# A fourth k-pair by seven block products in four of ten pairs of the second feed-forward's up stage, with a second k-pair's remainders there by ScalarE and adding DMAs

## The chip, the cores and the metric

The kernel runs on one NeuronCore of a Trainium2 chip. The metric is device time in microseconds (us) of one execution; the kernel before takes 2561.94 us, the median of three runs (2561.91 to 2562.84). A NeuronCore has a tensor engine (PE) for matmuls, a vector engine (DVE), a scalar engine (ACT), GpSimd (POOL) and SyncE (SP). Each runs its own instructions in order and waits on semaphores for the others. SP and POOL issue DMAs here; those of POOL can add to what lies at their destination.

## The reference

One layer of a diffusion backbone: a half-step SwiGLU, a mixing of tokens by attention and a long convolution, and another half-step SwiGLU, over 256 latent tokens (and 256 context tokens up to the mixing). The change is in the last SwiGLU, the second feed-forward:

```python
D_MODEL = 2048
SEQ = 256
D_FF = 5632

def swiglu(h, w_up, w_down):
    gate, up = jnp.split(h @ w_up, 2, axis=-1)
    return (jax.nn.silu(gate) * up) @ w_down

def half_ffn(s, m, slot, g, w_up, w_down):
    h = modulate(rms_norm(s, g), chunk(m, 3 * slot), chunk(m, 3 * slot + 1))
    return s + 0.5 * chunk(m, 3 * slot + 2) * swiglu(h, w_up, w_down)
```

All of it is in float32. Here `h` is 256 x 2048 and `w_up` 2048 x 11264.

## The kernel before

**Three matmuls for one.** The operands of PE are cast to `F32R`. To keep the precision, each operand x is split into a cast `hi` and a remainder `lo` = x - hi, and a product is hi·hi + lo·hi + hi·lo: three matmuls, added up in PSUM (`tok_mm`). The stationary operand is a 128 x 128 piece of the activations, the moving one 512 columns of weights. ACT makes the casts of the weights and DVE the remainders, in the order that `in_turn` writes down for each engine.

**The up stage.** The columns of `w_up` are taken in groups of 256 up columns with their 256 gate columns. Groups 0 and 1 come first, each alone (the loop `for g in range(2)`); the rest are ten pairs p = 1 to 10 of two groups. `plan` lists the pairs with their eight k-pairs q = 0 to 7 (a k-pair is 256 of the 2048 input rows), and after them the down stage. The loop over `plan` loads and splits the next k-pair's weights (`quad_of(*plan[n + 1])`) ahead of the matmuls of this one (`multiply`).

**Two ways to multiply a k-pair.** Plain: the tokens are two blocks of 128, the inner rows two, the columns two of 512; 8 block products of three matmuls, 24 in all. Block products (`is_summed`): seven in place of eight, 21 matmuls, of which some multiply sums of blocks. The sums of activation blocks are made once for each k-pair (`combine`, at group 1); those of weight blocks each time: `quad` subtracts in place in the raw tiles and then casts and takes remainders of four things, the first block (`first`, in the tiles `sq`, of which there is one pair), and `plain`, `odd` and `even` of two blocks each. Before, q = 2, 4 and 6 (`SUMMED`) are done so in pairs 1 to 10 (`SUM_PAIRS`). Four PSUM banks `mixed` hold products that enter several results; `collect` brings them together behind the last of these k-pairs, and `gated` applies the gate.

**Remainders by DMA.** For q = 1 of pairs 2 to 10 (argument `by_dma` of `quad`) DVE makes no remainder: ACT writes -hi into the tile `lo` (L1670), and a DMA issued by POOL adds the raw weights to it (L1671).

**Buffers.** The raw tiles (`raw`, `vraw`) are a ring of six, three k-pairs deep. The split tiles (`whi` and `wlo`, `vhi` and `vlo`) are a ring of five units; a plain k-pair takes two of them and one of block products three, beside the pair `sq`. A unit is filled again when PE has read the one five units back. The order of each engine's instructions is made by a scheduler that goes by when it believes operands to be ready; `in_turn` and `issue_after` bind it for casts and remainders of weights.

After the matmuls of q = 1 PE transposes the gated activations of the pair before (`turn_act`, L1598), which ACT and DVE split and, for some groups, POOL writes to DRAM (L1601, L1610).

Of the kernel before, what the change touches and what calls it, by code (L numbers as in the profile page):

```python
# [29 lines left out]
UPG = FF // 256  # L30
# [40 lines left out]
def hybrid_layer_kernel(ctx: ExitStack, tc: tile.TileContext, a):  # L71
# [20 lines left out]
    def tmp2(shape):  # L92
        return T(up, shape, "sg", bufs=3)
# [123 lines left out]
    def split(src, shape):  # L217
        hi, lo = U(shape, F32R), U(shape, F32R)
        S.copy(hi, src)
        V.tensor_sub(lo, src, hi.bitcast(F32))  # L220
        return hi, lo

    def split_to(src, hi, lo):
        S.copy(hi, src)
        V.tensor_sub(lo, src, hi.bitcast(F32))
        return hi, lo
# [1367 lines left out]
    def turn_act(g, at, bank=PB):  # L1594
# [8 lines left out]
        acts[g] = split(pt, (P, 2, L)) if g in SPILLED else split_to(pt, act_tile(), act_tile())  # L1603
        if g in DOWN_SUMMED[0]:
            m_ = tmp2((P, 2, L))
# [139 lines left out]
    for g in range(2):  # L1745
        ps = groups[g]
        behind = None
        if g == 0:
            for t in range(2):
                for ps_, ws_ in zip(groups, (ws, ws1)):  # L1750
                    for k in range(4):
                        tok_mm(ps_, [h[k][:, s, :] for s in range(2)], ws_[k], k == 0, False, (t,))
                if t == 0:
                    pt = turned(xn)
                    for d in range(4):
                        hi, lo = mod2(d, pt[:, d, :], h[d][:, :, P:L])
                        behind = behind or (lo, hi)
            rest_h(1)
        for kp in range(8):
            if kp < 2:  # L1760
                continue
            if g == 0 and kp == 2:
                pieces = ws[4:6]
            else:
                late = dict(zip(("behind", "behind_hi"), behind)) if g == 0 and kp < 6 else {}
                whi, wlo = weight(a["w_up2"][g, kp], (P, 2, 512), **late)
                pieces = [(whi[:, k2, :], wlo[:, k2, :]) for k2 in range(2)]
            for k2 in range(2):
                k = 2 * kp + k2
                tok_mm(ps, [h[k][:, s, :] for s in range(2)], pieces[k2], k == 0, k == KT - 1)  # L1770
            if g == 0 and kp in (2, 4):
                rest_h(kp // 2 + 1)
            if kp == 2 and prev:
                turn_act(*prev)
            if g == 0 and kp == 5:
                for t in range(2):
                    for b in range(NB):
                        nc.gpsimd.dma_start(xtd[t][b], xt[t][b])
            if g == 1 and kp in (3, 4, 5):
                combine(SUMMED[kp - 3])  # L1780
        at = U((P, 2, L))
        for t in range(2):
            sg = tmp2((P, L))
            S.activation(sg, ps[t][:, 0:L], AF.Silu)
            V.tensor_mul(at[:, t, :], ps[t][:, L : 2 * L], sg)
        prev = (g, at)
# [1 line left out]
    plan += [(UPG // 2 + bp, g) for bp in range(2) for g in DOWN_ORDERS[bp]]  # L1788

    def is_summed(p, q):  # L1790
        return q in DOWN_SUMMED[p - UPG // 2] if p >= UPG // 2 else p in SUM_PAIRS and q in SUMMED

    def quad_of(p, q):
        src = a["w_up2p"][p - 1] if p < UPG // 2 else a["w_dn2p"][p - UPG // 2]
        return quad([src[2 * q + k2] for k2 in range(2)], is_summed(p, q), p in SUM_PAIRS[1:] and q == 1)

    def fetch_next(at, count):

# [189 lines left out]
```

## Time and profile before

| | |
|---|---|
| median of three runs | 2561.94 us |
| profiled execution | 2561.77 us, span 2560.0 us |
| mean granted clock of PE | 0.997 |
| DVE | 2161.7 us busy, 84% |
| ACT | 1218.1 us busy, 48% |
| POOL | 367.1 us busy, 14% |

An engine's busy time is the union of its instructions; matmuls overlap, so a row's duration is longer than the distance to the next. In the table of stretches the span is cut at chosen times, here at the first matmuls of the pairs. In the chain of waits the last instruction is followed back to what released it. A timeline's row ends with a bracket where its engine was idle: how long, and whose end released it. "x2" joins two instructions of a kind that follow each other.

### The profile page before, as it was taken

What the parts mean: (1) busy time and instruction counts of PE and PEld (TensorE: products, weight loads), DVE (VectorE), ACT (ScalarE), POOL (GpSimd) and SP (SyncE); (2) the same over time, 40 slices, a digit from 0 to 9 for tenths busy, and PEclk for the clock granted to TensorE, in tenths of its full rate; (3) what the DMA queues carried; (4) which work ended last, traced back from release to release, by engine and by line L of the source; (5) the groups of instructions that cost most, each with busy time, mean ns of one, the idle gap of its engine ahead of it and who ended that gap; (6) DMA issues with size and microseconds to landing.
All of it is one profiled execution on the core that took longest, in us unless ns stands there. A gap on an engine that the chain in (4) does not pass through costs nothing.

```text
span 2560.0 us, 38554 instructions
## 1 busy us (share of the span) xinstructions
PE 2546.0 (99%) x14245; PEld 2191.0 (86%) x14245; DVE 2161.7 (84%) x3488; ACT 1218.1 (48%) x1710; POOL 367.1 (14%) x590
## 2 busy tenths in 40 slices
PE   8999999999999999999999999999999999999999
PEld 5678999999999999888888988888888888888887
DVE  6777888888888886777989797889789999999998
ACT  5454444444444443111211355567566666665554
POOL 1122222222222223320011000000000011012010
PEclk8999999999999999999999999999999999999999
DMA  9997888888888889996798556545747778789784
GB/s 362 389 284 221 250 243 254 242 245 243 252 247 256 245 251 314 395 372 204 257 333 294 187 158 183 161 127 164 250 160 238 232 255 256 245 256 315 235 286 158
DMA packets 209530, 641.27 MB, mean 250 GB/s; under 512 B 24603, under 2 KB 27644, under 8 KB 204988
## 3 DMA queue, kind: packets, MB, share of 16 engines
q1 hardware_dynamic: 134252, 481.84, 55.4%
q0 software_dynamic: 74896, 156.83, 23.7%
q8 instruction: 111, 1.82, 0.3%
q14 instruction: 79, 0.65, 0.1%
q10 hardware_dynamic: 192, 0.13, 0.0%
HBM read 559.25 MB, written 48.53 MB: 237 GB/s over the span
## 4 chain that ended last, share of the span: by engine, by line
PE 98%; DMA 1%; DVE 0%; ACT 0%; issue 0%; SPq 0%; ACTq 0%; DVEq 0%
PE pb L255 10%; PE pb L256 9%; PE pb L257 9%; PE pa L255 9%; PE pa L256 9%; PE pa L257 9%; PE pa L1418 6%; PE pa L1420 6%; PE pa L1419 6%; PE pb L1418 4%; PE pb L1420 4%; PE pb L1419 4%; PE pa L263 3%; PE pa L265 2%; PE pa L1105 1%; PE pa L1106 1%
## 5 line engine op out<-in xcount | busy, mean ns | idle before, releaser
L244 ACT CAST whi<-raw 128x1024 fp32r<-128x1024 f32 x233 | 245.1, 1052 | 480.9 <-PE pb L256 194.7
L248 DVE TENSOR_TENSOR wlo<-raw,whi 128x1024 fp32r<-128x1024 f32 x233 | 284.2, 1221 | 120.7 <-ACT whi L244 120.3
L255 PE MATMUL pa<-u,whi 128*128 128x256 f32 (+1 forms) x912 | 307.1, 337 | 2.1 <-ACT u L903 2.1
L256 PE MATMUL pa<-u,whi 128*128 128x256 f32 (+1 forms) x912 | 304.8, 334 | 0.4 <-DVE u L908 0.4
L257 PE MATMUL pa<-u,wlo 128*128 128x256 f32 (+1 forms) x912 | 304.5, 334 | 0.0
L255 PE MATMUL pb<-u,whi 128*128 128x256 f32 (+1 forms) x904 | 300.4, 332 | 0.0
L256 PE MATMUL pb<-u,whi 128*128 128x256 f32 (+1 forms) x904 | 298.5, 330 | 0.0
L257 PE MATMUL pb<-u,wlo 128*128 128x256 f32 (+1 forms) x904 | 298.3, 330 | 0.0
L467 ACT CAST bhi<-raw 128x768 fp32r<-128x768 f32 x111 | 92.5, 833 | 267.6 <-PE pb L256 131.8
L159 DVE CUSTOM_DVE_ANT_0 adas<-adaw,crow,cond 128x1024 bf16<-128x1024 f32 x160 | 204.9, 1280 | 14.3 <-DMA adaw<-in_w_adaT_dram 12.6
L159 DVE CUSTOM_DVE_ANT_0 adas<-adaw,crow,mod 128x1024 bf16<-128x1024 f32 x160 | 204.9, 1281 | 12.0 <-DMA adaw<-in_w_adaT_dram 10.0
L255 PEld LDWEIGHTS pa<-u,whi 128*128 128x128 f32 x912 | 173.1, 190 | 24.8 <-issue 4.1
L256 PEld LDWEIGHTS pa<-u,whi 128*128 128x128 f32 x912 | 173.5, 190 | 17.5 <-DVE u L908 1.5
L257 PEld LDWEIGHTS pa<-u,wlo 128*128 128x128 f32 x912 | 173.5, 190 | 17.1
L470 DVE TENSOR_TENSOR blo<-raw,bhi 128x768 fp32r<-128x768 f32 x111 | 106.2, 957 | 94.6 <-ACT bhi L467 94.4
L255 PEld LDWEIGHTS pb<-u,whi 128*128 128x128 f32 x904 | 171.8, 190 | 16.2 <-issue 0.7
L257 PEld LDWEIGHTS pb<-u,wlo 128*128 128x128 f32 x904 | 171.8, 190 | 15.6
L256 PEld LDWEIGHTS pb<-u,whi 128*128 128x128 f32 x904 | 171.9, 190 | 15.4
L278 ACT CAST whi<-raw 128x1024 fp32r<-128x1024 f32 x122 | 126.9, 1052 | 98.9 <-DVE raw L278 65.0
L1420 PE MATMUL pa<-whi,u 128*128 128x512 f32 x443 | 172.5, 389 | 0.0
L1418 PE MATMUL pa<-whi,u 128*128 128x512 f32 x442 | 172.5, 392 | 0.0
L1419 PE MATMUL pa<-wlo,u 128*128 128x512 f32 x442 | 172.2, 390 | 0.0
(473 smaller groups left out, 6673.5 us busy)
## 6 DMA issues: line engine op xcount, KB each, us to landing
adaw<-in_w_adaT_dram SPq DMA_DIRECT2D x224, 512.0 KB, 5.8
raw<-in_w_up1q_dram SPq DMA_DIRECT2D x124, 512.0 KB, 5.0
raw<-in_w_up2p_dram SPq DMA_DIRECT2D x107, 512.0 KB, 4.8
raw<-in_w_dn_dram SPq DMA_DIRECT2D x94, 512.0 KB, 5.6
u<-act POOLq DMA_DIRECT2D x172, 256.0 KB, 9.8
wrow<-in_w_ada_dram SPq DMA_DIRECT2D x32, 1024.0 KB, 10.9
raw<-in_w_dn2p_dram SPq DMA_DIRECT2D x59, 512.0 KB, 5.3
vraw<-in_w_up2p_dram SPq DMA_DIRECT2D x53, 512.0 KB, 5.0
```

The source lines that it names most:

```text
L159: V.tensor_tensor_reduce(out=sc, in0=t, in1=crow[i][:, b * (D // 2) : (b + 1) * (D // 2)], scale=1.0, scalar=mcol if b else bada[:, c * KT ...
L244: last_hi[0] = S.copy(hi, raw)
L248: last_lo[0] = V.tensor_sub(lo, raw, hi.bitcast(F32))
L255: PE.matmul(ps, w[0], xx[0], start=start, stop=False)
L256: PE.matmul(ps, w[0], xx[1], start=False, stop=False)
L257: return PE.matmul(ps, w[1], xx[0], start=False, stop=stop)
L278: return do(*args, **kw)
L467: return raw, hi, lo, S.copy(hi, raw[:, :, 0:3])
L470: return V.tensor_sub(lo, raw[:, :, 0:3], hi.bitcast(F32))
L1418: PE.matmul(ps[t], hi, w[0], start=start, stop=False)
L1419: PE.matmul(ps[t], hi, w[1], start=False, stop=False)
L1420: last = PE.matmul(ps[t], lo, w[0], start=False, stop=stop)
```

## The change

k-pair 5 joins 2, 4 and 6 in pairs 3, 5, 7 and 9, so that q = 4, 5 and 6 are block products one after the other there; `combine` makes its activation sums at group 1. In the same pairs the remainders of q = 3 are made by ACT and DMA, as those of q = 1 are.

```diff
+FOURTH, FOURTH_PAIRS = 5, range(3, 11, 2)
...
-            if g == 1 and kp in (3, 4, 5):
-                combine(SUMMED[kp - 3])
+            if g == 1 and kp in (3, 4, 5, 6):
+                combine((SUMMED + (FOURTH,))[kp - 3])
...
     def is_summed(p, q):
-        return q in DOWN_SUMMED[p - UPG // 2] if p >= UPG // 2 else p in SUM_PAIRS and q in SUMMED
+        return q in DOWN_SUMMED[p - UPG // 2] if p >= UPG // 2 else p in SUM_PAIRS and (q in SUMMED or q == FOURTH and p in FOURTH_PAIRS)
 
     def quad_of(p, q):
         src = a["w_up2p"][p - 1] if p < UPG // 2 else a["w_dn2p"][p - UPG // 2]
-        return quad([src[2 * q + k2] for k2 in range(2)], is_summed(p, q), p in SUM_PAIRS[1:] and q == 1)
+        return quad([src[2 * q + k2] for k2 in range(2)], is_summed(p, q), p in SUM_PAIRS[1:] and (q == 1 or q == 3 and p in FOURTH_PAIRS))
```

The new line near the top moves every line behind it down by one: L278 before is L279 after. The rows below show what stands in the engines' queues in pair 5. DVE before, from the last remainder of q = 4 through the two remainders of q = 5 to the chain of q = 6 (`sq` the first block, `raw` and `vraw` the raw tiles, `lo` tiles the remainders):

```order
L278 TENSOR_TENSOR vlo_21255<-raw_21246,vhi_21254 128x1024
L278 TENSOR_TENSOR vlo_21297<-raw_21292,vhi_21296 128x1024
L278 TENSOR_TENSOR wlo_21301<-vraw_21294,whi_21300 128x1024
L278 TENSOR_TENSOR sq_21330<-vraw_21325,sq_21329 128x512
L278 TENSOR_TENSOR vraw_21325<-vraw_21325 128x512
L278 TENSOR_TENSOR vraw_21325<-raw_21327,vraw_21325 128x512
L278 TENSOR_TENSOR wlo_21332<-raw_21327,whi_21331 128x1024
L278 TENSOR_TENSOR raw_21327<-raw_21327,vraw_21325 128x512
L278 TENSOR_TENSOR raw_21327<-raw_21327 128x512
L278 TENSOR_TENSOR wlo_21334<-vraw_21325,whi_21333 128x1024
L278 TENSOR_TENSOR vlo_21336<-raw_21327,vhi_21335 128x1024
```

DVE after, from the last remainder of q = 4 through the whole chain of q = 5 to the start of that of q = 6:

```order
L279 TENSOR_TENSOR vlo_21280<-raw_21271,vhi_21279 128x1024
L279 TENSOR_TENSOR sq_21322<-raw_21317,sq_21321 128x512
L279 TENSOR_TENSOR raw_21317<-raw_21317 128x512
L279 TENSOR_TENSOR raw_21317<-vraw_21319,raw_21317 128x512
L279 TENSOR_TENSOR wlo_21324<-vraw_21319,whi_21323 128x1024
L279 TENSOR_TENSOR vraw_21319<-vraw_21319,raw_21317 128x512
L279 TENSOR_TENSOR vraw_21319<-vraw_21319 128x512
L279 TENSOR_TENSOR wlo_21326<-raw_21317,whi_21325 128x1024
L279 TENSOR_TENSOR wlo_21328<-vraw_21319,whi_21327 128x1024
L279 TENSOR_TENSOR sq_21367<-vraw_21362,sq_21366 128x512
L279 TENSOR_TENSOR vraw_21362<-vraw_21362 128x512
L279 TENSOR_TENSOR vraw_21362<-raw_21364,vraw_21362 128x512
```

The two remainders between the chains are gone and eight instructions stand in their place; the three chains of q = 4, 5 and 6 touch each other.

PE before, the last rows of q = 6 in pair 5 (tiles `pa` and `pb` are PSUM banks, `u` activations and their sums):

```order
L1418 MATMUL pa_21209<-whi_21333,u_19509 128x512
L1419 MATMUL pa_21209<-wlo_21334,u_19509 128x512
L1420 MATMUL pa_21209<-whi_21333,u_19510 128x512
L1418 MATMUL pb_21083<-vhi_21335,u_19296 128x512
L1419 MATMUL pb_21083<-vlo_21336,u_19296 128x512
L1420 MATMUL pb_21083<-vhi_21335,u_19296 128x512
L1418 MATMUL pa_21208<-vhi_21335,u_19509 128x512
L1419 MATMUL pa_21208<-vlo_21336,u_19509 128x512
L1420 MATMUL pa_21208<-vhi_21335,u_19510 128x512
```

PE after, the same place:

```order
L1419 MATMUL pb_21106<-whi_21372,u_19296 128x512
L1420 MATMUL pa_21233<-vlo_21371,u_19509 128x512
L1421 MATMUL pa_21233<-vhi_21370,u_19510 128x512
L1420 MATMUL pa_21232<-vlo_21371,u_19509 128x512
L1421 MATMUL pa_21232<-vhi_21370,u_19510 128x512
L1419 MATMUL pa_21231<-whi_21372,u_19509 128x512
L1420 MATMUL pb_21106<-wlo_21373,u_19296 128x512
L1421 MATMUL pb_21106<-whi_21372,u_19296 128x512
L1420 MATMUL pa_21231<-wlo_21373,u_19509 128x512
L1421 MATMUL pa_21231<-whi_21372,u_19510 128x512
```

Before, each product's three matmuls stand together. After, the scheduler puts the ones that read only casts first, and the last four matmuls are those that come with the remainder of `even`.

ACT and POOL, for q = 3 of pair 5. ACT after, from the cast of its first tile to the cast of the first block of q = 4:

```order
L279 CAST whi_21238<-vraw_21234 128x1024
L1671 ACTIVATE wlo_21239<-whi_21238 128x1024
L279 CAST whi_21243<-raw_21236 128x1024
L220 CAST u_21200<-pa_21195 128x512
L1671 ACTIVATE wlo_21244<-whi_21243 128x1024
L1607 COPY sg_21204<-pa_21195 128x512
L279 CAST sq_21273<-raw_21269 128x512
```

POOL after, the DMAs of the same place (`wlo` the two that add; `sum` spilled activations of the pair before):

```order
L1672 DMA wlo_21239<-vraw_21234 128x1024
L1611 DMA sum_8_45_125<-u_21200 128x512
L1611 DMA sum_8_45_125<-u_21201 128x512
L1672 DMA wlo_21244<-raw_21236 128x1024
L1611 DMA sum_8_45_125<-u_21211 128x512
L1602 DMA act_9_40_120<-u_21224 128x512
```

The two rows L1671 on ACT and the two rows L1672 on POOL are new. The second adding DMA stands behind two spills.

## The prediction

> **What bounds the kernel now.** The page first: its span, its busy times, and the chain of waits that ended last.
>
> ```profile
> span 2560.0 us, 38554 instructions
> ...
> PE 2546.0 (99%) x14245; PEld 2191.0 (86%) x14245; DVE 2161.7 (84%) x3488; ACT 1218.1 (48%) x1710; POOL 367.1 (14%) x590
> ...
> PE 98%; DMA 1%; DVE 0%; ACT 0%; issue 0%; SPq 0%; ACTq 0%; DVEq 0%
> ```
>
> The tensor engine PE is busy in 99% of the span and makes up 98% of the chain, so an instruction taken off PE shortens the run, if the other engines can still feed PE. The change lies in the second feed-forward's up stage. I cut that stage into its weight pairs p (each 512 up columns with their gates); a table of stretches shows p = 4 and p = 5:
>
> ```profile
> 2029.04:2071.71 42.67, 42.67 (x192) 35.02 (x191) 38.92 (x52) 27.07 (x34) 2.88 (x5) 1.00 0.77 236
> 2071.71:2114.36 42.65, 42.65 (x193) 35.02 (x191) 38.94 (x52) 27.08 (x34) 5.00 (x9) 1.00 0.82 259
> ```
>
> Columns: length, then busy time and count of each engine, granted clock of PE, DMA share, GB/s. PE fills its stretch at full clock. VectorE (DVE) is busy for 38.94 us of 42.65: only 3.7 us are left, so DVE is the next bound, and the question is when its work falls due. The timelines of pair 5 tell that. PE's own rows, at the starts of the k-pairs q3 to q7 (the first, the third, and the last three) and two rows between:
>
> ```profile
> 2087.71 0.40 PE L1418 MATMUL pb<-vhi,u 128*128 128x512 f32 x1
> 2087.94 0.39 PE L1419 MATMUL pb<-vlo,u 128*128 128x512 f32 x1
> ...
> 2093.96 0.39 PE L1418 MATMUL pb<-whi,u 128*128 128x512 f32 x1
> ...
> 2095.77 0.39 PE L1420 MATMUL pa<-sq,u 128*128 128x512 f32 x1
> ...
> 2098.72 0.39 PE L1418 MATMUL pb<-vhi,u 128*128 128x512 f32 x1
> ...
> 2104.16 0.39 PE L1418 MATMUL pb<-whi,u 128*128 128x512 f32 x1
> ...
> 2108.92 0.39 PE L1418 MATMUL pb<-vhi,u 128*128 128x512 f32 x1
> ```
>
> Columns: start, duration, engine, line, operation, written tile and read tiles. The durations overlap: q4, a k-pair of block products with 21 matmuls, takes 2098.72 - 2093.96 = 4.76 us, and plain q5 with 24 takes 2104.16 - 2098.72 = 5.44 us. Both give 0.227 us for a matmul, not the 0.39 us in the row. 2095.77 is the last matmul that reads q4's tiles `sq` (the split of its first block).
>
> **The change, part by part.**
>
> *Matmuls.* In pairs 3, 5, 7 and 9 k-pair 5 has 21 matmuls in place of 24: 4 x 3 = 12 fewer, 12 x 0.227 = 2.7 us of PE. That is all that the change can bring: PE waits for nothing else in these stretches. It is also only half of 0.2% of the time (5.1 us), about the least that a measurement of this kernel can tell from no change.
>
> *VectorE.* A block-product k-pair costs DVE a fixed chain, here that of q6, made while PE works on q4 and q5; ahead of it stand two rows of q4's chain:
>
> ```profile
> 2086.16 0.69 DVE L278 TENSOR_TENSOR sq<-raw,sq 128x512 fp32r<-128x512 f32 x1 [0.45 <-ACT sq L278]
> ...
> 2093.75 2.36 DVE L278 TENSOR_TENSOR vlo<-raw,vhi 128x1024 fp32r<-128x1024 f32 x2
> ...
> 2097.16 0.68 DVE L278 TENSOR_TENSOR sq<-vraw,sq 128x512 fp32r<-128x512 f32 x1
> 2097.88 0.69 DVE L278 TENSOR_TENSOR vraw<-vraw 128x512 f32<-128x512 f32 x1
> 2098.60 0.69 DVE L278 TENSOR_TENSOR vraw<-raw,vraw 128x512 f32<-128x512 f32 x1
> 2099.21 1.22 DVE L278 TENSOR_TENSOR wlo<-raw,whi 128x1024 fp32r<-128x1024 f32 x1
> 2100.47 0.69 DVE L278 TENSOR_TENSOR raw<-raw,vraw 128x512 f32<-128x512 f32 x1
> 2101.19 0.69 DVE L278 TENSOR_TENSOR raw<-raw 128x512 f32<-128x512 f32 x1
> 2101.80 1.22 DVE L278 TENSOR_TENSOR wlo<-vraw,whi 128x1024 fp32r<-128x1024 f32 x1
> 2103.08 2.36 DVE L278 TENSOR_TENSOR vlo<-raw,vhi 128x1024 fp32r<-128x1024 f32 x2
> ```
>
> The eight instructions are the remainder of the first block (0.68 us), two subtractions, the remainder of `plain`, two subtractions, the remainders of `odd` and `even`. The last row holds two instructions of about 1.22 us, of which the first is `even` (2103.08 to 2104.30) and the second starts at 2103.08 + 2.36 - 1.22 = 2104.22. So a chain occupies DVE for 2104.22 - 2097.16 = 7.06 us, and its last result is there after 7.14 us, against 4.76 us of PE for the k-pair. A plain k-pair costs DVE two remainders, 2 x 1.22 = 2.44 us, and PE 5.44 us. Until now a plain k-pair stands between any two of blocks, and the two together need 7.06 + 2.44 = 9.5 us of DVE in 10.2 us of PE. After the change q4, q5 and q6 follow each other. Summed over the pair DVE would still do: 38.94 + 7.11 for q5 - 2.44 that q5 needed - 2.44 for q3's remainders = 41.2 us, beside 42.65 - 0.68 = 41.97 of PE. The order of the work does not allow it, because q5's chain can't begin early. The tiles `sq` exist once, and the cast that fills them is the first step of each chain, on ScalarE (ACT):
>
> ```profile
> 2080.07 1.06 ACT L278 CAST vhi<-vraw 128x1024 fp32r<-128x1024 f32 x1 [0.52 <-PE pb L1420]
> 2082.80 1.05 ACT L278 CAST whi<-raw 128x1024 fp32r<-128x1024 f32 x1 [1.67 <-PE pb L1420]
> ...
> 2085.50 0.62 ACT L278 CAST sq<-raw 128x512 fp32r<-128x512 f32 x1 [1.17 <-PE pa L1419]
> ...
> 2095.97 0.62 ACT L278 CAST sq<-vraw 128x512 fp32r<-128x512 f32 x1 [0.36 <-PE pa L1419]
> ...
> 2109.12 1.06 ACT L278 CAST vhi<-vraw 128x1024 fp32r<-128x1024 f32 x1 [0.30 <-PE pa L1420]
> 2110.21 1.06 ACT L1670 ACTIVATE vlo<-vhi 128x1024 fp32r<-128x1024 f32 x1
> ```
>
> The cast of 2095.97 waited for PE (the bracket) and started 2.01 us after q4 had (2093.96). This is the rule for each of them, as the table of waits for the stretch of these pairs shows (time in all, times, longest):
>
> ```profile
> ACT sq L278 <- PE pa L1419: 6.1, 8, 1.2
> ```
>
> From the cast to the chain's first instruction it is 2086.16 - 2085.50 = 0.66 us where DVE is free, and in the new order DVE is free then, since q4's last remainder is done at 2093.75 + 1.22 = 2094.97 and q5's plain remainders are gone. So in pair 5's times: cast of q5 2095.97, chain of q5 from 2096.63, chain of q6 straight behind it from 2103.69, its `even` remainder ready at 2103.69 + 7.14 = 2110.83. The order of PE, shown with the change, puts four matmuls of q6 behind that remainder: with 0.1 us for the signal (an estimate: from `odd` to `even` in the chain above it is 0.06 us, 2103.02 to 2103.08) and 4 x 0.227 us, q7 starts at 2111.84 in place of 2108.92. PE's 2.7 us are in this already. Inside it PE stands still four or five times for up to 1.2 us; which of these gaps is longest does not matter, as the sum is set by DVE's 14.2 us. **Term one: 2.92 us a pair, 4 x 2.92 = 11.7 us.**
>
> *After q6.* What DVE has lost, it makes up in q7 and in the next pair, which has 3.7 us to spare. q7's first remainder would be ready at 2110.75 + 1.22 = 2111.97, and is read at 2111.84 + 0.23: just in time, so at nothing; if not, tenths of a microsecond.
>
> *Remainders of q3 by ACT and adding DMAs.* ACT writes the negative of the cast into the remainder's tile (row 2110.21, L1670), and a DMA from GpSimd's queue adds the weights. ACT has the time (27.08 of 42.65 us busy). The length of the way from cast to landing is what counts. The trace has it for q1 of nine pairs, two each; one issue, and the times from issue to landing of all 18:
>
> ```profile
> 2111.57 0.88 POOL L1671 DMA_DIRECT2D vlo<-vraw  x1 [19.19 <-DVE u L1724]
> ```
>
> ```profile
> DMA to landing us min/median/max: 5.2/5.9/6.7
> ```
>
> From cast (2109.12) to issue it is 2.45 us, and 5.2 to 6.7, median 5.9 us more to the landing. q3's first cast waits until q1's first tile is read (bracket of the row of 2080.07), so it lands at 2080.07 + 2.45 + 5.9 = 2088.42. PE reads it with q3's second matmul, at 2087.94 (row above; 18 matmuls of q2 stand ahead of q3 in both orders). It is 0.48 us late: -0.2 with the shortest landing, 1.3 with the longest. I take 0.5. The second (cast 2082.80; with ACT's other work in between issued some 2.8 us later; in pairs 5 and 7 it stands on POOL's queue behind two DMAs that spill sums) lands at about 2091.6 and is read 16 matmuls after q3's first, 2087.71 + 0.5 + 3.6 = 2091.8: at nothing, bound 0 to 0.7. **Term two: 4 x 0.5 = 2.0 us, between 0 and 8.**
>
> The page "DMA: Bandwidth & Descriptors" of the Trainium skill (section "Anatomy of one DMA — SWDGE (gpsimd) path") fits 2.0 us plus bytes over 436 GB/s: an estimate of 3.2 us for these 512 KB. By it q3's tile would land at 2085.7, term two would be zero and the time 2573.5. The 18 landings, none under 5.2 us, disagree, and the sum goes by them.
>
> *Next pair's q1.* Its raw tiles are those of q6, free when q6's `odd` and `even` remainders are done. `odd` is now done 5.86 us into the chain (2103.02 - 2097.16), at 2109.55 in place of 2103.02. A load then takes 4.8 us, as the page's list of DMA issues has it:
>
> ```profile
> raw<-in_w_up2p_dram SPq DMA_DIRECT2D x107, 512.0 KB, 4.8
> ```
>
> With the same 8.35 us from cast to landing the first remainder is there at 2122.70; it is read after the next pair's q0, at 2111.84 + 2 x 5.44 + 0.23 = 2122.95. At nothing, bound 0.6 us a pair (longest landing).
>
> *k-pair 5's activations.* The new `combine` at g = 1 puts two additions, four of 128 columns and one remainder on DVE ahead of pair 1's weights. The first unit of pair 1 shows its place:
>
> ```profile
> 1898.48 1.21 DVE L1653 TENSOR_TENSOR wlo<-raw,whi 128x1024 fp32r<-128x1024 f32 x1
> 1899.62 0.28 DVE L1591 TENSOR_TENSOR u<-sg,u 128x128 f32<-128x128 f32 x1
> ```
>
> ```profile
> 1901.75 0.39 PE L1418 MATMUL pb<-whi,u 128*128 128x512 f32 x1
> ```
>
> Its remainder is done at 1899.70 and read at 1901.75 + 0.23; the additions (rows like the second one, 0.28 us for 128 columns) come to about 2 us, of which those ahead of this row take under 1. At nothing, bound 2 us once.
>
> **Sum:** 11.7 + 2.0 = 13.7 us. The profiled execution took 2561.77 us (span 2560.0 and 1.8 around it), 0.17 below the median of the runs shown. 2561.77 + 13.7 = 2575.5 us, 0.53% slower.
>
> **The rivals.**
>
> *DVE's work alone, without the hold of `sq`* (0.12). If q5's chain began as soon as DVE is free, 2094.97 in place of 2096.63, each pair would be 1.66 us shorter, and with the remainder of q3 in time 4 x (2.92 - 1.66) = 5.0 us remain: 2566.8. Against it stands the row of waits; for it, that nothing but this wait stands ahead of the chain: ACT has cast and DVE has subtracted all there is.
>
> *Not slower: nothing waits* (0.07). DVE's 41.2 us fit into 41.97, and PE gets its 2.7 us: 2559.1. It decides at the start of q5's chain: q6's `even` is wanted 4 matmuls before q7 would start without waits, at 2093.96 + 3 x 4.76 - 1.0 = 2107.2, so the two chains of 14.2 us must begin by 2093.0, 3.6 us before the time worked out above and ahead of q4's own last remainder (2094.97). Only if the tables overstate DVE's chain can this be.
>
> *The DMAs are late too* (0.18). Two more accumulating transfers a pair beside the loads, at a DMA share of 0.82: with the longest landing, 0.8 us more on q3's first remainder, 0.7 on the second, and 0.6 on the next pair's q1, 2.1 us a pair: 2575.5 + 8.4 = 2583.9.
>
> *The landing by the fit of 3.2 us* (0.03): 2573.5, as above.
>
> **How the numbers follow.** My forecast, DVE's two chains back to back, has 0.60, around 2571 to 2580 by the landing. The range of 2567 to 2585 takes in the late DMAs and most of the first rival, and leaves out the case without waits and the far ends. Faster by over 0.2% would take 5.1 us where only 2.7 can be had: 0.01. Within 0.2%, up to 2567.1, lie the case without waits and half of the first rival: 0.13. Slower by more: 0.86.
>
> **What the profile afterwards would show.** Pairs 3, 5, 7 and 9 last about 46.1 us and the others still 42.65; in the long ones PE idles before matmuls of q5 and q6, released by DVE's remainders or ACT's casts, and DVE runs without a gap from q5's chain to q6's end. If the long pairs last 42.0, DVE was not the bound; if they last longer than 47 with waits for DMAs before q3 or the next q1, the remainders by DMA were. The forecast is wrong in kind if time goes elsewhere: in pair 1, or in the down stage, whose work is unchanged.

## The result, and the profile after

| | median | fastest to slowest |
|---|---|---|
| before | 2561.91 us | 2559.97 to 2562.84 (5 runs) |
| changed | 2586.03 us | 2585.18 to 2589.51, and 3149.78 (5 runs) |

The ratio is 1.0094, with a 95% interval of 1.0082 to 1.0106: slower by 24 us, where 13.7 were forecast. The run of 3149.78 us, the profiled one, had a mean granted clock of 0.746, so the ratio leaves it out. The rows of "after" come from the same kernel profiled again as e1_as_changed (2584.53 us, ratio 1.0088, 1.0073 to 1.0103, clock 0.996).

Its page: the span, the busy times, and the chain that ended last.

```profile
span 2582.7 us, 38614 instructions
...
PE 2549.8 (99%) x14233; PEld 2185.9 (85%) x14233; DVE 2171.1 (84%) x3511; ACT 1230.2 (48%) x1727; POOL 373.8 (14%) x598
...
PE 90%; DMA 4%; DVE 3%; issue 1%; ACT 1%; POOL 0%; SPq 0%; ACTq 0%; POOLq 0%; DVEq 0%
```

Busy shares are as before; the chain tells the change. PE made up 98% of it and now makes up 90%, with DMAs and DVE in the difference. The table of stretches, cut at the first matmuls of pairs 3 to 10 (columns as in the prediction):

```profile
1987.73:2033.55 45.82, 43.19 (x189) 34.22 (x188) 38.99 (x53) 28.72 (x35) 4.54 (x6) 1.00 0.77 215
2033.55:2077.17 43.62, 43.23 (x192) 34.87 (x191) 40.91 (x55) 28.51 (x36) 2.96 (x5) 1.00 0.77 257
2077.17:2124.23 47.06, 43.41 (x189) 34.07 (x188) 39.00 (x53) 29.51 (x36) 6.71 (x10) 1.00 0.84 231
2124.23:2167.80 43.57, 42.97 (x193) 34.95 (x191) 40.59 (x55) 27.71 (x36) 5.07 (x9) 1.00 0.86 269
2167.80:2215.87 48.07, 43.41 (x190) 34.15 (x189) 38.99 (x53) 28.76 (x35) 6.68 (x10) 1.00 0.81 240
2215.87:2259.28 43.41, 43.19 (x193) 34.87 (x192) 40.92 (x55) 28.51 (x36) 2.95 (x5) 1.00 0.79 256
2259.28:2305.05 45.77, 43.19 (x190) 34.20 (x189) 39.02 (x53) 29.65 (x36) 4.53 (x6) 1.00 0.76 220
2305.05:2347.95 42.90, 42.90 (x193) 34.94 (x192) 39.42 (x53) 24.95 (x32) 12.58 (x23) 1.00 1.00 321
```

Three things are to be seen. Every pair had 42.65 us; of the four that the change makes (3, 5, 7 and 9, the long pairs from here on) 3 and 9 now have 45.8, close to the forecast's 46.1. Pairs 5 and 7 have 47.1 and 48.1, so they lose something that 3 and 9 don't. And pairs 4, 6 and 8, which the change does not touch, lose 0.8 to 1.0 us each. DVE's column says why that can be: its work in a long pair was reckoned at 41.2 us, but only 39.0 are done inside the pair, and the next does 40.9 where 38.9 were usual. Two microseconds of each long pair's work are carried over.

### The profile page after: what moved, and what is told of

It is laid out like the page before. It is cut to its first block, busy times and chain, and to the rows that moved or that the text cites. A ratio compares the mean times of both kernels' runs of the same rounds, so it can differ in the third digit from the quotient of the medians.

```text
span 3148.0 us, 38614 instructions
## 1 busy us (share of the span) xinstructions
PE 3135.8 (100%) x14233; PEld 2413.9 (77%) x14233; DVE 2188.3 (70%) x3511; ACT 1237.2 (39%) x1727; POOL 373.8 (12%) x598
## 4 chain that ended last, share of the span: by engine, by line
PE 98%; DVE 1%; ACT 0%; issue 0%; POOL 0%; ACTq 0%; DVEq 0%; POOLq 0%
PE pb L257 10%; PE pb L258 9%; PE pb L256 9%; PE pa L256 9%; PE pa L258 9%; PE pa L257 9%; PE pa L1420 6%; PE pa L1419 6%; PE pa L1421 6%; PE pb L1419 4%; PE pb L1420 4%; PE pb L1421 4%; PE pa L264 3%; PE pa L266 2%; PE pb L199 1%; PE pa L1106 1%
## 5 line engine op out<-in xcount | busy, mean ns | idle before, releaser
L256 PE MATMUL pa<-u,whi 128*128 128x256 f32 (+1 forms) x912 | 351.5, 386 | 2.1 <-ACT u L904 2.1
L258 PE MATMUL pa<-u,wlo 128*128 128x256 f32 (+1 forms) x912 | 351.7, 386 | 0.0
L257 PE MATMUL pa<-u,whi 128*128 128x256 f32 (+1 forms) x912 | 349.7, 384 | 0.3 <-DVE u L909 0.3
L256 PE MATMUL pb<-u,whi 128*128 128x256 f32 (+1 forms) x904 | 344.1, 381 | 0.0
L257 PE MATMUL pb<-u,whi 128*128 128x256 f32 (+1 forms) x904 | 342.7, 379 | 0.0
L258 PE MATMUL pb<-u,wlo 128*128 128x256 f32 (+1 forms) x904 | 342.3, 379 | 0.0
L256 PEld LDWEIGHTS pa<-u,whi 128*128 128x128 f32 x912 | 191.6, 210 | 46.5 <-issue 7.5
L1420 PE MATMUL pa<-wlo,u 128*128 128x512 f32 x483 | 220.6, 457 | 0.0
L258 PEld LDWEIGHTS pa<-u,wlo 128*128 128x128 f32 x912 | 191.7, 210 | 37.4 <-issue 0.5
L1421 PE MATMUL pa<-whi,u 128*128 128x512 f32 x484 | 220.0, 455 | 0.0
L257 PEld LDWEIGHTS pa<-u,whi 128*128 128x128 f32 x912 | 192.0, 210 | 36.6 <-issue 2.0
L1419 PE MATMUL pa<-whi,u 128*128 128x512 f32 x483 | 219.9, 458 | 0.0
L256 PEld LDWEIGHTS pb<-u,whi 128*128 128x128 f32 x904 | 191.3, 212 | 35.3 <-issue 1.9
L258 PEld LDWEIGHTS pb<-u,wlo 128*128 128x128 f32 x904 | 190.2, 210 | 34.5 <-issue 1.3
L257 PEld LDWEIGHTS pb<-u,whi 128*128 128x128 f32 x904 | 190.4, 211 | 34.1 <-issue 0.3
L279 ACT CAST whi<-raw 128x1024 fp32r<-128x1024 f32 x122 | 127.3, 1049 | 135.9 <-DVE raw L279 69.6
```

The costliest lines, as they stand in the source:

```text
L256: PE.matmul(ps, w[0], xx[0], start=start, stop=False)
L257: PE.matmul(ps, w[0], xx[1], start=False, stop=False)
L258: return PE.matmul(ps, w[1], xx[0], start=False, stop=stop)
L279: return do(*args, **kw)
L1419: PE.matmul(ps[t], hi, w[0], start=start, stop=False)
L1420: PE.matmul(ps[t], hi, w[1], start=False, stop=False)
```

## Where the time went

**q5 and q6 (four pairs).** Pair 3 in the order of the prediction: ACT's cast of q5's first block (and, last in q6, that of `even`), the ends and the joint of DVE's two chains, and PE from q4's first matmul to q7's, with the three waits between.

```profile
2012.09 0.62 ACT L279 CAST sq<-raw 128x512 fp32r<-128x512 f32 x1 [2.51 <-PE pa L1420]
...
2024.60 2.00 ACT L279 CAST whi<-vraw 128x1024 fp32r<-128x1024 f32 x2 [1.05 <-DVE vraw L279]
```

```profile
2012.75 0.69 DVE L279 TENSOR_TENSOR sq<-raw,sq 128x512 fp32r<-128x512 f32 x1 [1.91 <-ACT sq L279]
...
2018.65 1.23 DVE L279 TENSOR_TENSOR vlo<-raw,vhi 128x1024 fp32r<-128x1024 f32 x1
2019.79 0.68 DVE L279 TENSOR_TENSOR sq<-raw,sq 128x512 fp32r<-128x512 f32 x1
...
2025.68 2.36 DVE L279 TENSOR_TENSOR wlo<-vraw,whi 128x1024 fp32r<-128x1024 f32 x2
```

```profile
2010.08 0.39 PE L1419 MATMUL pb<-vhi,u 128*128 128x512 f32 x1
...
2018.67 0.50 PE L1419 MATMUL pb<-vhi,u 128*128 128x512 f32 x1 [0.92 <-ACT vhi L279]
...
2023.12 0.50 PE L1419 MATMUL pa<-whi,u 128*128 128x512 f32 x1 [0.71 <-ACT whi L279]
...
2025.70 0.51 PE L1419 MATMUL pb<-whi,u 128*128 128x512 f32 x1 [0.92 <-ACT whi L279]
...
2028.11 0.39 PE L1419 MATMUL pb<-whi,u 128*128 128x512 f32 x1
```

The cast starts 2.01 us after q4 (forecast 2.01), the chain 0.66 later (0.66), DVE having stood idle for 1.91 us. It runs without a gap for 7.04 us to the first row of q6's chain, whose `even` remainder is done at 2025.68 + 1.22 = 2026.90. From q4 to q7 it is 18.03 us, forecast 17.88, before 14.96. What PE waits for by name is ACT, not DVE: casts of `odd` and `even`, which themselves wait for DVE's subtractions (the second row of ACT). The last wait ends with the cast of q6's `even`, ten matmuls ahead of q7; the `even` remainder, from which the prediction reckoned q7's start, is done at 2026.90 and was read at 2027.18, so PE no longer waited for it.

**q3's remainders (pairs 5 and 7).** POOL in pair 5, which starts at 2077.17: the first adding DMA (L1672), two DMAs that spill sums (L1611), the second adding DMA; then the time from issue to landing of that second one, and PE's wait for it.

```profile
2087.97 0.86 POOL L1672 DMA_DIRECT2D wlo<-vraw  x1 [9.98 <-ACT wlo L1671]
2090.08 0.56 POOL L1611 DMA_DIRECT2D sum<-u  x1 [1.25 <-ACT u L220]
2090.81 0.55 POOL L1611 DMA_DIRECT2D sum<-u  x1 [0.16 <-issue]
2091.40 0.89 POOL L1672 DMA_DIRECT2D wlo<-raw  x1
```

```profile
DMA to landing us min/median/max: 6.7/6.7/6.7
```

```profile
2098.13 0.50 PE L1420 MATMUL pb<-wlo,u 128*128 128x512 f32 x1 [1.07 <-DMA wlo<-raw]
```

The first was issued 10.80 us into the pair (forecast 10.81) and came in time after 5.3 us. The second was issued 14.23 us into the pair, 0.4 later than in pairs 3 and 9, which have no spill here, and landed at 2091.40 + 6.7 = 2098.1, just as PE goes on; in pairs 3 and 9 it took 4.8 us. In pair 7 it is the first that PE waits for. It took 7.3 us, without a spill ahead of it, and in that stretch other transfers were slow too: the two loads issued 1.7 and 2.9 us ahead of it took 6.6 us each (4.4 to 4.7 in pairs 3, 5 and 9), and q1's two adding DMAs 7.6 and 7.4 (5.4 to 6.3).

```profile
2185.95 0.50 PE L1420 MATMUL pb<-vlo,u 128*128 128x512 f32 x1 [1.92 <-DMA vlo<-raw]
```

From q2's start to q4's the four pairs take 0.1, 1.3, 2.3 and 0.0 us longer than before.

**The next pair's q1 (pairs 4, 6, 8).** All that these pairs lose lies in q1, which lasts 7.0 to 7.2 us in place of 6.24. ACT and POOL at the start of pair 4 (2033.55), and PE's wait for q1's second remainder there:

```profile
2031.41 1.05 ACT L279 CAST whi<-vraw 128x1024 fp32r<-128x1024 f32 x1
2034.47 0.42 ACT L1740 ACTIVATE sg<-u 128x256 f32<-128x256 f32 x1 [2.01 <-DVE u L1737]
2034.80 1.05 ACT L1671 ACTIVATE wlo<-whi 128x1024 fp32r<-128x1024 f32 x1
```

```profile
2031.80 0.89 POOL L1672 DMA_DIRECT2D wlo<-raw  x1 [25.10 <-PE pb L1421]
2036.14 0.89 POOL L1672 DMA_DIRECT2D wlo<-vraw  x1 [3.46 <-ACT sg L1740]
```

```profile
2042.78 0.50 PE L1420 MATMUL pa<-wlo,u 128*128 128x512 f32 x1 [0.20 <-DMA wlo<-vraw]
```

Between the cast of q1's second tile and its negation (L1671) stands an activation of the pair's gate (L1740). It waits 2.01 us for an addition (L1737) that DVE, in arrears, does late. So ACT, then POOL, issue q1's second DMA 2.59 us after the pair's start, against 0.07 us ahead of the start of pair 3, and it lands 9.2 us into the pair. In pair 8 it is the same (issued 2.61 us in). In pair 6 it is not: there the negation stands right behind the cast, the DMA is issued only 0.75 us after the start, but takes 8.4 us from issue to landing (5.3 to 5.7 in pairs 4, 6 and 8 before):

```profile
2124.98 0.89 POOL L1672 DMA_DIRECT2D wlo<-raw  x1 [1.52 <-ACT wlo L1671]
```

```profile
2133.38 0.50 PE L1420 MATMUL pa<-wlo,u 128*128 128x512 f32 x1 [0.60 <-DMA wlo<-raw]
```

The first of q1's DMAs is issued 1.0 to 1.8 us ahead of the pair, before it was 2.79, and takes 6.6 to 7.7 us; in pair 4 PE waits 0.2 us for it as well. So the loss has two parts, a later issue and a longer landing.

**The start of the down stage.** Here a gate's activation behind a waiting cast costs 2.3 us once. ACT, DVE and PE:

```profile
2351.31 1.05 ACT L279 CAST vhi<-vraw 128x1024 fp32r<-128x1024 f32 x1 [1.83 <-DMA vraw<-in_w_dn2p_dram]
2352.26 1.03 ACT L1740 ACTIVATE sg<-u 128x256 f32<-128x256 f32 x3
```

```profile
2352.71 0.76 DVE L1741 TENSOR_TENSOR u<-u,sg 128x256 f32<-128x256 f32 x2 [1.55 <-ACT sg L1740]
```

```profile
2364.91 0.50 PE L1419 MATMUL pa<-whi,u 128*128 128x512 f32 x1 [2.31 <-DVE u L226]
```

A cast waits for a load of down weights, the gate's activations stand behind the cast, DVE waits for them, and its remainders of the last activations come late for PE.

The account of e1: 4 x 3.07 = 12.3 us in q5 and q6; q3 0.1 + 1.3 + 2.3 + 0.0, which is 3.8 before rounding; pairs 4, 6 and 8 together 2.6; pair 10 and all behind it 277.69 - 275.01 = 2.7. That is 21.4 of the 21.9 us between the medians (2584.53 - 2562.63).

## The experiments

All times are medians; "before" was 2561.66 to 2562.96 us beside these runs. The pair lengths are the distances between the pairs' first matmuls in the profiled run of each kernel, the last column is from pair 10's first matmul to the end of the span.

| kernel | us | ratio (95%) | 3 | 4 | 5 | 6 | 7 | 8 | 9 | 10 to end |
|---|---|---|---|---|---|---|---|---|---|---|
| before | | | 42.66 | 42.67 | 42.65 | 42.66 | 42.68 | 42.64 | 42.64 | 275.01 |
| e1_as_changed | 2584.53 | 1.0088 (1.0073-1.0103) | 45.82 | 43.62 | 47.06 | 43.57 | 48.07 | 43.41 | 45.77 | 277.69 |
| e2_products_only | 2577.10 | 1.0060 (1.0043-1.0077) | 45.77 | 43.43 | 45.77 | 42.89 | 45.77 | 43.05 | 45.74 | 276.09 |
| e3_remainders_only | 2566.50 | 1.0018 (1.0008-1.0027) | 42.62 | 42.67 | 44.23 | 42.68 | 45.14 | 42.66 | 42.98 | 275.15 |
| e4_no_hold | 2575.31 | 1.0053 (1.0038-1.0068) | 43.87 | 43.50 | 44.89 | 43.07 | 44.69 | 43.41 | 43.87 | 279.59 |
| e5_no_hold_products | 2571.20 | 1.0040 (1.0027-1.0054) | 43.99 | 43.21 | 44.03 | 44.29 | 44.03 | 43.08 | 44.17 | 276.41 |
| e6_spills_behind | 2564.15 | 1.0008 (1.0000-1.0017) | 42.75 | 42.65 | 42.81 | 42.66 | 42.64 | 42.66 | 42.64 | 274.88 |
| e7_next_q1_by_dve | 2589.30 | 1.0112 (1.0098-1.0126) | 45.73 | 43.69 | 47.96 | 43.37 | 48.63 | 42.99 | 48.68 | 279.55 |
| e8_short_chain | 2568.91 | 1.0032 (1.0019-1.0044) | 43.50 | 43.12 | 43.47 | 43.65 | 43.50 | 43.73 | 43.52 | 276.29 |
| e9_all_spills_behind | 2581.34 | 1.0077 (1.0063-1.0090) | 46.42 | 43.57 | 45.79 | 43.30 | 47.16 | 43.44 | 45.91 | 278.88 |
| e10_relieved | 2590.21 | 1.0111 (1.0098-1.0125) | 43.84 | 47.57 | 43.86 | 49.59 | 43.84 | 48.63 | 43.85 | 279.94 |
| e11_three_pairs | 2575.67 | 1.0055 (1.0042-1.0068) | 45.73 | 43.15 | 47.51 | 43.37 | 47.26 | 43.49 | 42.68 | 274.83 |
| e12_pool_subtracts | 2584.18 | 1.0083 (1.0070-1.0097) | 47.22 | 43.55 | 47.21 | 43.46 | 47.21 | 43.07 | 47.22 | 276.04 |

### The two halves of the change, and the hold

e1 is the change again. e2 takes q3's remainders back to DVE:

```diff
-... p in SUM_PAIRS[1:] and (q == 1 or q == 3 and p in FOURTH_PAIRS))
+... p in SUM_PAIRS[1:] and q == 1)
```

e3 keeps them with ACT and the DMAs and drops the fourth k-pair of block products:

```diff
-            if g == 1 and kp in (3, 4, 5, 6):
+            if g == 1 and kp in (3, 4, 5):
...
-        return ... p in SUM_PAIRS and (q in SUMMED or q == FOURTH and p in FOURTH_PAIRS)
+        return ... p in SUM_PAIRS and q in SUMMED
```

The hold is the wait of q5's first cast until PE has read the `sq` tiles of q4. e4 is the whole change with tiles of its own for q5's first block, so that it has no hold; the order on all engines is the same:

```diff
-        first = tuple(T(up, (P, 512), "sq", F32R, 2) for _ in range(2))
+        first = tuple(U((P, 512), F32R) if spare else T(up, (P, 512), "sq", F32R, 2) for _ in range(2))
```

(`spare` is q == FOURTH and p in FOURTH_PAIRS.) Expected:

> The changed kernel once more, for a profile at full clock. Theory A (two DVE chains back to back behind the hold of `sq`, q3's remainder by DMA half a microsecond late): pairs 3, 5, 7 and 9 last 46.1 us by the prediction's sum, which is 3.4 us each; the measured 24 us are some 6.0 us each, so A asks for 48.7 us if its mechanism holds and a term was too small. Theory B (DMAs late beyond that): 48.7 us too, but with waits before q3 or before the next pair's q1 that a DMA ends, 3 us or more in a pair. Theory C (elsewhere): the four pairs last about 46 us, and 10 us are lost in pair 1, the even pairs or the down stage.

> k-pair 5 as block products, but q3's remainders by DVE as before. A: q3 is not late, the two chains remain; at 2.9 us a pair 2573.6 us, and up to 4 us a pair more if DVE, now with 43.6 us of work in 42 us, can't be done by the next pair. B: the waits on DMAs go, and with them most of the loss: 2566 us or less. C: unchanged from the changed kernel, 2586 us.

> q3's remainders by ACT and DMA, k-pair 5 plain as before. A: only q3 comes late, 0.5 us a pair, 2564 us, between 2562 and 2570. B: the DMAs are late here too, 3 us a pair: 2574 us. C: 2562 us.

> The changed kernel, where the first block of k-pair 5 gets tiles of its own in place of `sq`; every engine's order is the same. A: q5's chain starts when DVE is free and not 2 us behind q4's start: 1.66 us less in each of the four pairs, 2579.4 us. B and C: no change, 2586 us.

Neither half alone explains 22 us: the products cost 14.5 (2577.10 - 2562.63; 2573.6 was theory A's time), the remainders by DMA 3.9 (2566.50, within A's range). Their sum is 3.5 us short of e1. By the profiles the long pairs do not make this up: pairs 4, 6 and 8 and all from pair 10 on lose 2.7 us more in e1 than in e2 and e3 together. In e2 all four long pairs have 45.8 us, as pairs 3 and 9 of e1 have. So q3's two remainders, taken off DVE, gave it nothing: in e2 too it stands idle ahead of q5's chain (1.68 us in pair 3, 1.91 in e1) until the first block is cast. e3 loses its time in pairs 5 and 7, and 0.3 us in pair 9, not 0.5 us in each of four. Without the hold, e4's q5 has no stall left (4.76 us from its first matmul to q6's), q6 keeps 0.6 to 1.7 us, and the kernel is 9.2 us faster than e1, at 2575.31 where theory A expected 2579.4. That is so although its time from pair 10 on is 1.9 us longer. ACT's table of waits shows the hold in e1 over pairs 3 to 9, four waits; e4's has no such row:

```profile
ACT sq L279 <- PE pa L1420: 13.1, 4, 4.4
```

### Is it the hold, the chain, the spills, or the next q1?

e5 is e4's edit with e2's. e8 is e2 with the four subtractions left out of q5's split in the long pairs (where `short` is true), so its products of sums are not those of the layer:

```diff
-        in_turn("dve", V.tensor_sub, b11, b12, b11)
+        short or in_turn("dve", V.tensor_sub, b11, b12, b11)
```

and so for the other three. e6 is e3 with the spilling DMAs issued behind both adding ones:

```diff
-                nc.gpsimd.dma_start(sumd2[g][:, s_], t.rearrange("p a b -> p (a b)"))
+            spills.extend((sumd2[g][:, s_], t) for ...)
...
+        if place == 2:
+            while spills:
+                d_, t_ = spills.pop(0)
+                then(added[0], nc.gpsimd.dma_start, d_, t_.rearrange("p a b -> p (a b)"))
```

(`added[0]` is the last adding DMA, and `then` puts a DMA behind it.) e7 is the whole change with q1's remainders by DVE in pairs 4, 6, 8 and 10:

```diff
-... (q == 1 or q == 3 and p in FOURTH_PAIRS)
+... (q == 1 and p - 1 not in FOURTH_PAIRS or q == 3 and p in FOURTH_PAIRS)
```

> Block products for k-pair 5 with q3's remainders by DVE as before the change, and the first block of k-pair 5 in tiles of its own, so that its cast need not wait until PE has read q4's first block. DVE's work is the same as in e2_products_only (odd pairs 45.77 us there, against 42.65 before the change). Theory A (the two chains stand behind the hold of the first block's tiles): in the run of the whole change without the hold q5 lost its stall and q6 kept 0.6 to 1.7 us, so the odd pairs fall to 42.7 to 43.7 us, the even ones stay at 43.2, and the time is 2565 to 2569 us. Rival D (DVE's sum of work sets the pace, the hold does not matter): the odd pairs stay at 45 us or more and the time at 2575 to 2577.

> The remainders of q3 by ACT and adding DMAs in pairs 3, 5, 7 and 9 with no fourth k-pair of block products, as in e3_remainders_only, but on POOL's queue the DMAs that spill sums in pairs 5 and 7 stand behind both adding DMAs in place of two of them ahead of the second. Nothing else changes its order. In e3 the second adding DMA took 6.9 and 7.8 us from issue to landing in pairs 5 and 7 and 4.9 and 5.1 in pairs 3 and 9, and pairs 5 and 7 lasted 44.2 and 45.1 us. Theory S (the two spills ahead of it slow it down): its landing falls to about 5 us, pairs 5 and 7 to 42.7 to 43.2 us, the time to about 2562.6 to 2563.6. Rival L (the loads of those pairs or the streamed sums slow it, not the spills): pairs 5 and 7 stay above 44 us and the time at 2566.

> The whole change, but in pairs 4, 6, 8 and 10, those that follow a long one, the remainders of q1 are made by DVE in place of ACT and adding DMA. These pairs lost 0.25 to 1.0 us each in e1, 2.9 us in all, with PE waiting for the DMA of q1's remainder. Theory N (the raw tiles come free late, so that cast, DMA and landing come late, while DVE's part would be in time): the four pairs fall to 42.7 us and the time from 2584.5 to about 2581.6. Rival D (DVE itself has not made up its arrears there): with 2.44 us more for DVE the pairs stay at 43.5 us or above, and the time at 2584 to 2588.

> As e2_products_only (fourth k-pair of block products, q3's remainders by DVE), with the four subtractions between weight blocks left out of k-pair 5's split, in the four pairs: DVE's chain for q5 is 4 x 0.72 = 2.9 us shorter, and PE, ACT's casts and the loads are the same. Theory A (DVE's two chains back to back set q7's start): q5's chain ends before q6's first block can be cast (q5's start + 2.67 us), so q6's even remainder is ready 4.76 + 2.67 + 7.14 = 14.57 us after q4's start and q7 starts 15.6 us after it, in place of 18.0: 2.4 us less a pair, odd pairs 43.3 us, time about 2567. Rival C (ACT's casts, whose ends released PE in most of these waits, set the pace by themselves): 18.0 us and 2577 stay.

*e5:* the hold is worth 45.76 - 44.05 = 1.7 us in a long pair, which is the 1.66 us of the prediction's first rival. What is left, 1.4 us (1.2 in pairs 3 and 9 of e4), was more than the 0.1 to 1.1 expected here; the prediction's first rival left 2.92 - 1.66 = 1.26. The time is later too (2571.2, not 2565 to 2569): pairs 4, 6 and 8 lose 0.4 to 1.6 us, and 1.4 are lost from pair 10 on.

*e8:* with 2.9 us less in DVE's chain the long pairs have 43.5 us, 0.2 over theory A, and of e2's three waits of PE in pair 3 one is left:

```profile
PE pb L1419 <- ACT whi L279: 0.9, 1, 0.9
```

ACT's casts, which PE waits for by name, are as many as in e2; with DVE's chain shorter they come in time. Rival C falls. (PE takes the matmuls of q5 and q6 in another order than in e2, as the scheduler made it.) The even pairs got no shorter, which A had not promised: they lose 2.5 us together, in e2 1.4. DVE's work in a long pair is 2.9 us less, but its first addition for the gate stands 0.8 us ahead of pair 4, as in e1 and e2, where it was 1.8 before. So the arrears at a long pair's end do not follow the sum of DVE's work.

*e6:* pairs 5 and 7 are back at 42.8 and 42.6 us. POOL in pair 7, the second adding DMA with the spills behind it, and its landing:

```profile
2171.75 0.88 POOL L1672 DMA_DIRECT2D vlo<-raw  x1 [2.21 <-PE pa L1420]
2172.47 1.27 POOL L279 DMA_DIRECT2D sum<-u  x2
```

```profile
DMA to landing us min/median/max: 4.8/4.8/4.8
```

4.8 us, against 7.8 for the same DMA in e3, and 4.9 against 6.9 in pair 5. So two spills of 256 KB ahead of it on the queue cost it 2 to 3 us on its way, beside 0.4 for its later issue. Other traces agree: with the spills ahead, in e1, e4 and e11, this DMA takes 6.7 to 7.7 us in pairs 5 and 7; with the spills behind, in e9, e10 and e12, 4.8 to 5.3, but 6.3 in pair 7 of e9. This is theory S in the traces. The times say less: the median of 2564.15 is 0.5 us above what S expected, some runs reached 2566.67, which the one profiled run does not explain, and the intervals of e3 and e6 overlap.

*e7:* theory N fell. Pairs 4, 6 and 8 lost 1.0, 0.7 and 0.4 us, in e1 1.0, 0.9 and 0.8, and in pairs 4 and 6 PE now waits for DVE's remainder (0.7 us in pair 4), so DVE is short there. But rival D does not hold as it stood either: only pair 4 is above its 43.5 us, and the time (2589.3) is beyond its range. The growth lies in the long pairs behind (48.0, 48.6 and 48.7 us in pairs 5, 7 and 9), and there not in DVE's chains: q5 and q6 last as long as in e1. PE's waits in pair 9, all of them:

```profile
PE pb L1420 <- DMA vlo<-raw: 2.1, 1, 2.1
PE pb L1419 <- ACT whi L279: 0.9, 1, 0.9
PE pb L1419 <- ACT vhi L279: 0.9, 1, 0.9
PE pa L1419 <- ACT whi L279: 0.7, 1, 0.7
PE pb L1420 <- DMA vlo<-vraw: 0.5, 1, 0.5
```

The three waits for ACT are e1's; the two for adding DMAs, of q3 and of q1, are new. q3's first DMA is issued 0.7 to 1.1 us later than in e1 in pairs 5, 7 and 9 and takes 6.5 to 7.5 us, q1's take 8.0 to 8.9. Why they land so late was not tried.

### Do the losses add up, and can it be mended?

e9 is the whole change with e6's edit. e10 is e4 with e6's edit and q0's remainders by DMA in pairs 4, 6, 8 and 10 (`q == 0 and p - 1 in FOURTH_PAIRS`). e11 leaves out pair 9 (`FOURTH_PAIRS = range(3, 9, 2)`). e12 is e10 without q0's DMAs, and with q5's four subtractions on POOL in the long pairs:

```diff
-        in_turn("dve", V.tensor_sub, b11, b12, b11)
+        in_turn(*side, b11, b12, b11)
...
+        side = ("pool", G.tensor_sub) if spare else ("dve", V.tensor_sub)
```

> The whole change, with the spilling DMAs of pairs 5 and 7 behind both adding DMAs on POOL's queue, as in e6_spills_behind. Theory S + A (the two losses are separate: DVE's chains, and the adding DMAs behind the spills): pairs 5 and 7 fall from 47.06 and 48.07 us to the 45.8 of pairs 3 and 9, 3.5 us in all, and the time from 2584.5 to about 2581; the even pairs keep their 43.4 to 43.6. Rival (with the pairs already late from DVE, q3's wait is no loss of its own, or turns up again in q5 and q6): pairs 5 and 7 stay at 47 us and the time above 2583.

> A version meant to lose least: the whole change with the first block of k-pair 5 in tiles of its own, the spills behind the adding DMAs, and in the even pairs 4, 6, 8 and 10 also the remainders of q0 by ACT and adding DMAs, which takes 2 x 1.22 = 2.4 us off DVE where it makes up its arrears. Theory D (what is left without the hold is DVE's arrears, carried from one pair to the next): pairs 3, 5, 7 and 9 last 43.9 us or a little less (43.87 in pairs 3 and 9 of e4_no_hold), the even ones fall from 43.1 to 43.5 to 42.7 to 42.9, and the time is 2566 to 2569 us. Rival L (the adding DMA of q0 lands late, or holds the raw tiles): the even pairs stay above 43.2 us or grow, with PE waiting on the DMA ahead of q0, and the time is 2572 or more. Beating the kernel before would take odd pairs under 42.65.

> The whole change in three pairs, 3, 5 and 7, in place of four; pairs 9 and 10 are as before the change. In e1 the last pair and the down stage together took 2.7 us longer than before, 2.3 of them one wait of PE for the remainder of an activation in the first of the down stage's products. Theory T (that wait comes from DVE's and ACT's arrears of pair 9, carried through pair 10): from pair 10's start to the end it is 275.0 us again, pair 9 lasts 42.65 and pair 10 what it did before, and the time is 2584.5 - 3.1 - 2.7 = 2578.7. Rival U (it comes from where buffers and queues stand after the change, whatever pair 9 does): the wait of about 2 us stays and the time is 2581.

> A version meant to beat both: the whole change with the first block of k-pair 5 in tiles of its own and the spills behind the adding DMAs (both as in e10_relieved, without its DMAs for q0), and the four subtractions of k-pair 5's split on POOL in place of DVE, 4 x 0.72 = 2.9 us off DVE in each long pair. No run shows what a subtraction of 128 x 512 costs on POOL; 0.69 us on DVE is the nearest row. Theory D (DVE's arrears are what is left without the hold): the long pairs fall from the 43.85 us of e10 to 42.0 (three matmuls fewer and no wait) to 42.7, the even ones from 43.4 to 42.7, and the time is 2559.5 to 2564; it beats the kernel before only at the lower end. Rival P (POOL takes several times DVE's duration, or slows DVE beside it, so that q5's casts come late): PE waits for casts of q5, the long pairs last 45 us or more and the time is over 2572.

*e9:* 2581.34 against 2581 expected, though not quite as expected. Pair 5 fell from 47.06 to 45.79 us, pair 7 only to 47.16: there the two adding DMAs took 6.8 and 6.3 us with no spill ahead of them, in a stretch in which q1's took 7.9 and 7.6 and the two loads ahead of them 5.7 and 5.9. What made them slow there, in e9 as in e1, was not tried. Pair 3, which has no spill, was 0.6 us longer than in e1, at a wait for q3's first adding DMA.

*e10:* the long pairs have 43.85 us, evenly (pairs 5 and 7 had 44.9 and 44.7 in e4, with the spills ahead), but the even ones 47.6 to 49.6. Rival L was right: q0's first DMA is issued 3.6 us ahead of the pair and lands 7.5 us later. PE's wait in pair 4:

```profile
PE pa L1420 <- DMA vlo<-raw: 3.6, 1, 3.6
```

*e11:* without the long pair 9 the time from pair 10 to the end is 274.83 us, the wait of 2.3 us is gone, and 2575.67 us is 8.9 less than e1 (5.8 were expected; pairs 4 and 7 were 0.5 and 0.8 us shorter by themselves). That is theory T's sign. But the arrears of pair 9 are not enough for the wait: e2, e5 and e8 have the long pair 9 too and lose at most 0.3 us at this place. PE's waits in e2 from pair 10 to the end, all of them:

```profile
PE pa L1420 <- DMA vlo<-vraw: 0.5, 1, 0.5
```

The load for which ACT's cast waits is issued as late in e2, e5 and e8 (37.1 to 37.3 us into pair 10; 36.4 in e1, 35.2 before), but takes 7.4 to 7.7 us, where it takes 9.6 to 9.9 in e1, e4 and e9, the three kernels with this wait, of 2.2 to 2.5 us. So a late issue alone does not make the wait, and the long landing comes with it; what makes the landing long was not tried.

*e12:* POOL's subtractions, of operands in one tile and in two:

```profile
L279 POOL TENSOR_TENSOR raw<-raw 128x512 f32<-128x512 f32 x5 | 10.8, 2168 | 9.4 <-DVE u L279 9.1
L279 POOL TENSOR_TENSOR raw<-raw,raw 128x512 f32<-128x512 f32 x4 | 5.2, 1290 | 0.3
```

2.17 and 1.29 us, where DVE takes 0.69 for either. The four last 2 x 2.17 + 2 x 1.29 = 6.9 us and stand behind one another ahead of q5's casts and remainders; the long pairs have 47.2 us. Rival P was right. DVE did little beside them: in each long pair one remainder of 1.22 us, as elsewhere, and one of 1.33.

No version beats the kernel before. Each long pair without the hold keeps 1.2 us of loss where three matmuls would give 0.68 us of gain.

## Why the prediction was wrong, point by point

- **Direction and matmuls.** Right: 12 matmuls fewer (14245 to 14233 on PE), no gain left of them.
- **Term one, 11.7 us.** Right in mechanism and nearly in size: 12.3 us. Its steps, the cast 2.01 us after q4, 0.66 to the chain, 14.2 us of DVE, held to within 0.05 us. Of its details, PE idles three times, not four or five, and what releases it last is the cast of `even` and not the remainder; the two come to q7's start within 0.3 us of each other, so that the size was met in part by luck. Rival one (no hold) priced the hold rightly too, by e5, and what is left without it by e4.
- **Term two, 2.0 us: too small by half, and not where it was put.** It gave 0.5 us to q3's first remainder in each pair and took the second "at nothing, bound 0 to 0.7". The issues came as forecast to 0.03 us in pairs 3 and 9, and there the landings of 4.8 to 5.5 us left nothing to wait for. In pair 5 the second, noted as standing behind two spills, took 6.7 us, and in pair 7 the first took 7.3: 3.8 us in all. The step that failed is that the range of 18 landings, 5.2 to 6.7 us, would hold for new DMAs with other neighbours. For the one behind the spills e3 and e6 show the cause; for the slow first one in pair 7 it stays open, but the loads beside it were slow too.
- **"Next pair's q1. At nothing, bound 0.6 us a pair."** Failed: 0.8 to 1.0 us in pairs 4, 6 and 8, 2.6 in all. The step priced the first of q1's two tiles only, with "the same 8.35 us from cast to landing". The raw tiles were free in time for the cast to start 3.5 to 4.2 us ahead of the pair (2.9 by the prediction), but from cast to landing it was 9.1 to 10.2 us for the first tile and 10.4 to 11.3 for the second, on which PE waits. In pairs 4 and 8 a gate's activation that waits for DVE stands ahead of the second tile's negation; in pair 6 it is chiefly the landing that is long (8.4 us). This is read from e1's trace; e7 shows that DVE is short there, and no run took the gate's activation out of ACT's way.
- **"What DVE has lost, it makes up in q7 and in the next pair, which has 3.7 us to spare."** This step failed, and with it the two terms beside it that stood at nothing. A spare of 3.7 us in 42.65 was an average. DVE does make the 2 us up in the next pair (40.9 us in place of 38.9), but not before other engines have waited for it.
- **The down stage, left at nothing:** 2.7 us with pair 10, gone in e11. By the prediction's own sign this is time gone elsewhere, in a stage whose work is unchanged. It takes a late load of down weights that also lands late; why it lands late stays open.
- **`combine` at g = 1, at nothing:** right, pair 1 lasts 41.97 us as before and PE waits for nothing ahead of it. (e1 starts it 1.3 us later than the profile of before, but so does e3, which lacks the new `combine`; pair 3 starts at 1985.3 to 1988.1 us in the twelve profiles.)
- **The rivals.** "The DMAs are late too" has the nearest time, 2583.9, but by other terms: it put q3's waits into all four long pairs, where two have them, and q1's at a longer landing alone, where the issue is late too. That it comes so near is luck. The landing by the fit of the Trainium skill's page "DMA: Bandwidth & Descriptors" (section "Anatomy of one DMA — SWDGE (gpsimd) path"), an estimate of 3.2 us for 512 KB by its formula, is not seen: the adding DMAs of e1 took 4.8 to 8.4 us, median 6.3.

Against the runs beside it e1 lost 21.9 us, 8.2 more than forecast; of these 0.6 lie in term one, 1.8 in term two, and 2.6 and 2.7 in the next pair and the down stage, which were priced at nothing. The step that failed most is therefore that DVE's arrears, and what they do to the DMAs behind them, cost nothing after q6.

## What to carry to other kernels

A spare time that is an average over a stage does not pay arrears at once: follow them through each engine's queue up to the first instruction of another engine that waits, here a gate's activation on ACT with a remainder's negation behind it. A transfer's landing time is to be taken from transfers with the same neighbours on their queue; two spills moved behind an adding DMA gave it 2 to 3 us back. Where one tile is held by the matmuls of the step before, work taken off the engine behind it was worth nothing (e1 against e2, pairs 3 and 9), and without the hold only 0.1 to 0.3 us (e4 against e5); a second tile was worth 1.6 to 2.0 us in such a pair.

## What was not expected of the hardware

An accumulating DMA of 512 KB from GpSimd's queue took 4.8 to 5.5 us from issue to landing in the middle of pairs 3 and 9 of e1, 6.7 to 7.8 us behind two writes of 256 KB (pairs 5 and 7 of e1, e3, e4 and e11), and 7.5 to 9.6 us at the start of pair 4 in e10, where four follow each other within 7.2 us. A subtraction on POOL of 128 x 512 in float32 took 1.29 us with operands in two tiles and 2.17 us with both in one, where DVE took 0.69 us for both.
